# The forget gate's four columns computed with the first query chunk of the third layer

## The chip, the cores and the metric

The kernel runs on one core of one Trainium2 chip. The metric is the device time of one launch in microseconds (us), the median of the runs. Engines are named as the profile names them: PE is TensorE's matmul, PEld its load of the stationary operand, DVE is VectorE, ACT is ScalarE, POOL is GpSimd, SP is SyncE, which here only issues DMAs. ACTq and SPq are the DMA issues of those two queues.

## What is computed

Four transformer layers follow one another on 512 tokens of 1024 features, in float32. The change touches the third, called the even layer. Cut to what matters, its reference is:

```python
hn = rms_norm(h, norm_g)                       # [512, 1024]
proj = hn @ w_in                               # qa ka va qb kb vb, f_logit (4 columns), z
qa, ka = rope(rms_norm(qa)), rope(rms_norm(ka))
oa = diff_attention(qa..., ka..., va, lam)
cum_logf = cumsum(log_sigmoid(f_logit + b_forget), axis=1)
ob = fox_attention(norm(qb), norm(kb), vb, cum_logf)   # scores get cum_logf[q] - cum_logf[k]
h = h + (concat(rms_norm(oa), ob) * silu(z)) @ w_out
```

`f_logit` is four of the 4100 columns of the projection, one for each head of `fox_attention`. Only the second half of the layer's attention uses what is made of it.

## The kernel before

Every product is made of three TensorE passes (`mm3`, L236): both operands are split into a rounded part and a remainder, and high x high, high x low and low x high are summed in PSUM. Weights come in chunks of 256 columns. `weights` (L210) loads a chunk with two DMAs of 512 KB on SP into one of three `raw` buffers, and splits it in four pieces of two feature blocks: ACT makes `wh`, DVE or POOL makes `wl`. There are 8 `wh` and 8 `wl` buffers, so two chunks fit.

`quad` (L269) computes a chunk for all 512 tokens with the tokens stationary: 4 token tiles x 8 feature blocks x 3 passes = 96 matmuls of 256 moving columns into one PSUM buffer `A`. There are two `A` buffers of two banks each, and four single banks: three with the tag `B`, one with the tag `F`. `proj_tok` (L242) runs the token tiles outermost unless `step` is given; with `step=1` the feature blocks are outermost. `head_norm` (L165) copies the sums to SBUF on ACT and normalises each head, `rope` (L185) rotates.

`even` (L1289) opens with constants in `lp`, the layer's pool, whose memory was used before it by the pools of the stage ahead (`xr1`, `plv`). Then `proj_group` (L1095) makes chunk q, chunk k, chunk v and two gate blocks (`gates2`) one after another, each in the next `A` buffer; `forget` (L1115) makes the forget gate; four groups of attention follow, with the next `proj_group` as filler work for PE. The gate blocks are computed features-stationary with 512 moving columns.

`forget` loads its 1024 x 4 weights on ACT's queue, splits them, and runs 8 feature blocks x 3 passes = 24 matmuls with 4 stationary columns and 512 moving ones into bank `F`, which leaves the four heads on four partitions. A chain of ACT and DVE instructions and a scan along the tokens follows, a store of the sums to DRAM for the second half, and four transposes.

The stage ahead is the end of layer two: `w_out` adds its output to the residual in two pairs of token tiles, `feat_pair` (L392) normalises and transposes each pair into `h2h` and `h2l` (the operands of chunk q), and `ple_values` (L1367) computes 2 chunks x 4 token tiles x 6 = 48 matmuls of 512 columns in banks `F` and `B`, copies each result out (`pv`, two buffers, in pool `plv`) and stores it to DRAM (`pw_d`, L1385).

The order of the work on each engine is not written by hand. A scheduler takes the instructions in program order as their priority, and moves one ahead when it is ready earlier; each engine then runs its list in order. A pool whose memory overlaps an earlier pool's waits until the earlier one is released.

Of the kernel before, what the change touches and what calls it, by code (L numbers as in the profile page):

```python
# [9 lines left out]
F32 = mybir.dt.float32  # L10
F32R = mybir.dt.float32r
# [18 lines left out]
class Kern:  # L30
# [38 lines left out]
    def A(self):  # L69
        return self.tl(self.ps, [128, 1024], "A", 2)  # L70
# [91 lines left out]
        self.nc.scalar.activation(out=t, in_=ps, func=AF.Tanh, scale=0.5)  # L162
        self.nc.vector.scalar_tensor_tensor(out=out, in0=t, scalar=1.0, in1=ps, op0=ALU.add, op1=ALU.mult)

    def head_norm(self, ps, H, d):  # L165

        nc = self.nc
        T = ps.shape[1]
        if T == 4:
            x = self.T4([128, T, H * d])  # L170
            nc.scalar.copy(out=x, in_=ps)
            ps = x
        sq = self.T4([128, T, H * d])
        nc.scalar.activation(out=sq, in_=ps, func=AF.Square, scale=d ** -0.5)
        ss = self.sml(T * H)
        nc.vector.tensor_reduce(out=ss.rearrange("p (t h) -> p t h", t=T),
                                in_=sq.rearrange("p t (h d) -> p t h d", d=d), axis=AX.X, op=ALU.add)
        r = self.rstd(ss, T * H)
        xn = ps.rearrange("p t (h d) -> p t h d", d=d)
        nc.vector.tensor_tensor(out=xn, in0=xn,  # L180
                                in1=r.rearrange("p (t h) -> p t h", t=T).unsqueeze(3).to_broadcast([128, T, H, d]),
                                op=ALU.mult)
        return xn
# [678 lines left out]
    def mla_load(self, pool, src):  # L862
        G = self.mla_tiles(pool, 1, 2)
        for x, d in zip((G[0], G[1], f32(G[2])), src):
            self.nc.sync.dma_start(out=x, in_=d)
        return G

    def mla_attn(self, box, att, G, g, g_d, gT):
        st = {}

        def stacks(e):
            q, k, _ = G[g]
            st[e] = [self.qk_any(lambda t: x[:, t, e, :], 6, 96, self.tl(box["mat"], [96, 2, 768], "qk", 4, F32R))
# [5 lines left out]
        def gate(e, pr):  # L879
# [4 lines left out]

        items = self.dense_items(score, lambda e, j: G[g][2][:, j, e].rearrange("p e d -> p (e d)"), gate,
                                 lambda pr: gT[g][:, 256 * pr:256 * pr + 256], att, g == 3)
# [197 lines left out]
        nc.gpsimd.tensor_copy(out=C[:, :, rot:d], in_=g[:, rot:d].unsqueeze(1).to_broadcast([128, 4, d - rot]))  # L1084
        return C, S, rot

    def proj_heads(self, X, W, out, d, tab):

        xn = self.head_norm(self.quad(X, W, 256), 256 // d, d)
        if isinstance(tab, tuple):  # L1090
            self.rope(out, xn, tab[0], tab[1], 0, tab[2])
        else:
            self.gain_heads(out, xn, tab)

    def proj_group(self, X, w, cols, pool, d, tq, tk, z):  # L1095

        H = 256 // d
        q = self.tl(pool, [128, 4, H, d], "q")
        k = self.tl(pool, [128, 4, H, d], "k")
        v = self.tl(pool, [128, 4, 2, 2, 128], "v", 2, F32R)  # L1100
        self.proj_heads(X, self.weights(w[cols[0]]), q, d, tq)
        self.proj_heads(X, self.weights(w[cols[1]]), k, d, tk)
        self.v_split(v, self.quad(X, self.weights(w[cols[2]]), 256).rearrange("p t (h d) -> p t h d", h=2))
        if z is not None:
            self.gates2(X, self.weights(w[cols[3]]), z)
        return q, k, v
# [5 lines left out]
            nc_ = self.nc.vector if b else self.nc.gpsimd  # L1112
            nc_.tensor_tensor(out=z[b], in0=z[b], in1=t, op=ALU.mult)

    def forget(self, X, fp, cq, nc_d):  # L1115
        nc, I = self.nc, self.I
        wf = fp.tile([128, 8, 4], F32, name="wf")
        nc.scalar.dma_start(out=wf, in_=I["w_forget"])
        wfh, wfl = fp.tile([128, 8, 4], F32R, name="wfh"), fp.tile([128, 8, 4], F32R, name="wfl")
        self.split(wf, wfh, wfl)  # L1120
        bf = fp.tile([4, 1], F32, name="bf")
        nc.scalar.dma_start(out=bf, in_=I["b_forget_2"])
        p = self.B()
        for k in range(8):
            self.mm3(p[0:4, :], wfh[:, k, :], wfl[:, k, :], X[0][:, k, :], X[1][:, k, :], k == 0, k == 7)
        f, e, cum = (self.T4([4, 512]) for _ in range(3))
        nc.vector.tensor_scalar(out=f, in0=p[0:4, :], scalar1=bf, scalar2=None, op0=ALU.add)
        nc.scalar.activation(out=e, in_=f, func=AF.Abs)
        nc.scalar.activation(out=e, in_=e, func=AF.Exp, scale=-1.0)
        nc.scalar.activation(out=e, in_=e, func=AF.Ln, bias=1.0)  # L1130
        nc.vector.tensor_scalar(out=f, in0=f, scalar1=0.0, scalar2=None, op0=ALU.min)
        nc.vector.tensor_tensor(out=f, in0=f, in1=e, op=ALU.subtract)
        nc.vector.memset(e, 1.0)
        nc.vector.tensor_tensor_scan(out=cum, data0=e, data1=f, initial=0.0, op0=ALU.mult, op1=ALU.add)
        nc.vector.tensor_scalar(out=f, in0=cum, scalar1=-1.0, scalar2=None, op0=ALU.mult)
        nc.sync.dma_start(out=nc_d, in_=f)
        pc = self.B()
        for t in range(4):
            nc.tensor.transpose(out=pc[:, 4 * t:4 * t + 4], in_=cum[:, 128 * t:128 * t + 128], identity=self.ident[0:4, 0:4])
        nc.vector.tensor_copy(out=cq, in_=pc[:, 0:16])  # L1140
# [148 lines left out]
    def even(self, X, close_x, lp, zt, fold, nc_d):  # L1289
        nc, I = self.nc, self.I  # L1290
        w = I["even_w"]
        gq = self.gain_row(lp, "qn_a_2", "gqa", 0.125)
        gk = self.gain_row(lp, "kn_a_2", "gka")
        te = self.rot_table(lp, 0)
        TQ = self.partial_tables(lp, te, gq, 16, 64)
        TK = self.partial_tables(lp, te, gk, 16, 64)
        gqb = self.gain_row(lp, "qn_b_2", "gqb", float(np.float32(128 ** -0.5)))
        gkb = self.gain_row(lp, "kn_b_2", "gkb")
        li = 0.8 - 0.6 * math.exp(-0.3 * 0)
        sub = self.gain_row(lp, "subln_g_2", "sub", (1.0 - li) * 0.5)  # L1300
        cm = lp.tile([128, 512], F32, name="cmask")
        nc.scalar.dma_start(out=cm, in_=I["causal"])
        cq = lp.tile([128, 16], F32, name="cq")
        nlam = self.lam(lp)
        zg = lambda g: zt[2 * g:2 * g + 2]
        cols = lambda g: [c + g for c in (0, 2, 4, 12)] if g < 2 else [c + g - 2 for c in (6, 8, 10, 14)]
        with self.filler(True):
            G = self.proj_group(X, w, cols(0), lp, 64, TQ, TK, zg(0))
        self.forget(X, lp, cq, nc_d)
        for g in range(4):  # L1310
            if g < 2:
                self.pipeline(self.diff_items(G, lp, cm, nlam, sub, zg(g)))
                fold(*((0, 1) if g == 0 else (2,)))
            else:
                nck = {}

                def bias(h, i, g=g, nck=nck):
                    if h not in nck:
                        nck[h] = self.tl(lp, [128, 512], "nck", 2)
                        hh = 2 * (g - 2) + h  # L1320
                        nc.sync.dma_start(out=nck[h], in_=nc_d[hh:hh + 1, :].to_broadcast([128, 512]))
                    n = 128 * (i + 1)
                    b = self.T4([128, n])
                    c = 4 * i + 2 * (g - 2) + h
                    nc.scalar.activation(out=b, in_=nck[h][:, 0:n], func=AF.Identity, bias=cq[:, c:c + 1])
                    nc.gpsimd.tensor_tensor(out=b[:, n - 128:n], in0=b[:, n - 128:n], in1=cm[:, 384:512], op=ALU.add)
                    return b

                self.pipeline(self.causal_items(G, lp, zg(g), bias, True))
            if g < 3:  # L1330
                with self.filler(True):
                    G = self.proj_group(X, w, cols(g + 1), lp, 64 if g < 1 else 128, TQ if g < 1 else gqb,
                                        TK if g < 1 else gkb, zg(1) if g < 1 else None)
        with self.filler(True):
            for g in (2, 3):
                self.late_gates(X, self.weights(w[12 + g]), zg(g))
        close_x()
# [419 lines left out]
def chunks(w, n=256):  # L1757

    K, N = w.shape
    return np.ascontiguousarray(w.reshape(K // 128, 128, N // n, n).transpose(2, 1, 0, 3))  # L1760


def layout(inp):
    A = np.ascontiguousarray
# [4 lines left out]
    d = {}  # L1769
# [20 lines left out]
    cols = np.concatenate([heads(512, 2, p64), np.arange(640, 768), heads(0, 8, p64), np.arange(768, 3328)])  # L1790
# [2 lines left out]
    d["conv_w"] = A(g["conv_w"][0].reshape(3, 4, 128).transpose(2, 1, 0))  # L1793
    ev = g["w_in_even_2"][0]
    d["even_w"] = chunks(np.concatenate([ev[:, 0:3072], ev[:, 3076:4100]], 1))
    d["w_forget"] = A(ev[:, 3072:3076].reshape(8, 128, 4).transpose(1, 0, 2))
    d["b_forget_2"] = A(g["b_forget_2"].reshape(4, 1))
    d["even_wo"] = chunks(g["w_out_even_2"][0])
    d["odd_w"] = chunks(g["w_in_odd_2"][0])
# [14 lines left out]
    z = np.zeros((128, 128), f)  # L1814
# [28 lines left out]
```

## Time and profile before

| | |
|---|---|
| median of 3 runs | 1543.21 us (1541.46 to 1546.2) |
| the profiled execution | 1542.88 us, span 1541.1 us |
| granted TensorE clock, mean | 0.991 |
| PE / PEld / DVE / ACT / POOL busy | 96% / 89% / 67% / 55% / 36% of the span |
| DMA | 168.20 MB, mean 109 GB/s |

Matmuls are pipelined: the length of one in the profile (0.39 us for 512 columns) is longer than the distance to the next one's start (0.23 us), so what PE can do is read from start to start. Shares of busy time hide short idle stretches; where it matters, starts are read one by one.

### The profile page before, as it was taken

How to read it: one execution, taken by the hardware profiler on the slowest of the kernel's cores; microseconds unless marked ns; L12 is line 12 of the kernel's file. 1: busy time of each engine (PE TensorE's matmuls, PEld its weight loads, DVE VectorE, ACT ScalarE, POOL GpSimd, SP SyncE). 2: the span in 40 equal slices, each digit the busy share in tenths (PEclk: the TensorE clock that was granted, in tenths of full speed). 3: DMA queues.
4: the chain of work that ended last, by engine and by line, in shares of the span. 5: the costliest groups of instructions: out<-in, count | busy, mean ns of one | idle time of the engine just before them, and what ended most of it. 6: DMA issues, size and time to landing. Idle time of an engine off the chain costs nothing.

```text
span 1541.1 us, 28602 instructions
## 1 busy us (share of the span) xinstructions
PE 1483.3 (96%) x10760; PEld 1367.7 (89%) x10760; DVE 1039.1 (67%) x2123; ACT 845.0 (55%) x1759; POOL 551.4 (36%) x650
## 2 busy tenths in 40 slices
PE   5999999989999989999999999999999999999998
PEld 3789888877998989888889989998899989998998
DVE  6777887888886377777755358887644456555544
ACT  6545555689997154465653446566533534454422
POOL 1533534567675024222322244335301244443100
PEclk8999999999999999999999999999999999999999
DMA  8343564121120431222334432112434431222323
GB/s 308 116 131 120 185 207 157 45 104 33 63 70 25 153 119 66 96 97 83 102 129 149 136 114 92 61 56 96 144 103 148 139 105 69 69 71 78 126 90 110
DMA packets 60685, 168.20 MB, mean 109 GB/s; under 512 B 9890, under 2 KB 18530, under 8 KB 60546
## 3 DMA queue, kind: packets, MB, share of 16 engines
q1 hardware_dynamic: 54768, 163.52, 31.1%
q10 hardware_dynamic: 5778, 2.84, 0.7%
q8 instruction: 85, 1.39, 0.4%
q14 instruction: 54, 0.44, 0.1%
HBM read 144.06 MB, written 22.28 MB: 108 GB/s over the span
## 4 chain that ended last, share of the span: by engine, by line
PE 81%; DVE 7%; ACT 4%; DMA 3%; issue 2%; POOL 2%; ACTq 0%; SPq 0%; DVEq 0%; POOLq 0%
PE A L240 17%; PE A L238 17%; PE A L239 16%; PE B L524 3%; PE F L238 3%; PE F L239 3%; PE F L240 3%; PE F L595 2%; PE B L238 2%; PE B L239 2%; PE B L240 2%; DVE wl L232 2%; PE B L996 1%; PE B L388 1%; PE B L1168 1%
## 5 line engine op out<-in xcount | busy, mean ns | idle before, releaser
L229 ACT CAST wh<-raw 128x512 fp32r<-128x512 f32 (+1 forms) x380 | 227.1, 615 | 220.9 <-PE A L240 147.3
L232 DVE TENSOR_TENSOR wl<-raw,wh 128x512 fp32r<-128x512 f32 (+1 forms) x316 | 230.7, 744 | 99.2 <-ACT wh L229 96.6
L481 POOL TENSOR_SCALAR P<-P,s 128x768 f32<-128x768 f32 (+3 forms) x192 | 151.4, 794 | 183.0 <-DVE s L1264 37.5
L144 DVE TENSOR_TENSOR PTl<-B,PTh 128x512 fp32r<-128x512 f32 (+2 forms) x208 | 127.9, 632 | 43.9 <-ACT PTh L143 31.4
L232 POOL TENSOR_TENSOR wl<-raw,wh 128x512 fp32r<-128x512 f32 x64 | 87.3, 1365 | 155.8 <-ACT wh L229 139.2
L138 POOL TENSOR_TENSOR s8f<-s8f,mhalf 128x4 f32<-128x4 f32 (+2 forms) x53 | 61.5, 1161 | 221.0 <-DVE s8f L137 122.2
L143 ACT CAST PTh<-B 128x512 fp32r<-128x512 f32 (+2 forms) x208 | 108.2, 545 | 58.1 <-PE B L524 26.8
L238 PE MATMUL A<-wh,mh 128*128 128x256 f32 x480 | 136.6, 285 | 2.9 <-ACT mh L143 2.9
L239 PE MATMUL A<-wl,mh 128*128 128x256 f32 x480 | 136.0, 284 | 0.0
L240 PE MATMUL A<-wh,g 128*128 128x256 f32 x408 | 115.6, 285 | 1.4 <-DVE g L144 1.4
L238 PE MATMUL A<-wh,h4h 128*128 128x256 f32 x384 | 109.1, 285 | 0.0
L239 PE MATMUL A<-wl,h4h 128*128 128x256 f32 x384 | 108.9, 284 | 0.0
L240 PE MATMUL A<-wh,h4l 128*128 128x256 f32 x384 | 108.8, 285 | 0.0
L240 PE MATMUL A<-wh,h2l 128*128 128x256 f32 x384 | 108.1, 283 | 0.0
L238 PE MATMUL A<-wh,h2h 128*128 128x256 f32 x384 | 108.0, 282 | 0.0
L239 PE MATMUL A<-wl,h2h 128*128 128x256 f32 x384 | 108.0, 282 | 0.0
L238 PEld LDWEIGHTS A<-wh,mh 128*128 128x128 f32 x480 | 92.0, 192 | 4.2 <-ACT mh L143 3.3
L239 PEld LDWEIGHTS A<-wl,mh 128*128 128x128 f32 x480 | 91.9, 192 | 0.1
L524 PE MATMUL B<-ident,P 128*128 128x128 f32 x592 | 86.3, 274 | 4.5 <-DVE PTl L144 2.4
L240 PEld LDWEIGHTS A<-wh,g 128*128 128x128 f32 x408 | 78.0, 192 | 1.8 <-DVE g L144 1.8
L490 ACT ACTIVATE P<-A,s 128x768 f32<-128x768 f32 (+1 forms) x96 | 73.2, 765 | 7.4 <-DVE s L488 4.7
L524 PEld LDWEIGHTS B<-ident,P 128*128 128x128 f32 x592 | 67.5, 141 | 9.1 <-POOL P L481 2.5
(523 smaller groups left out, 4927.3 us busy)
## 6 DMA issues: line engine op xcount, KB each, us to landing
raw<-mod_w SPq DMA_DIRECT2D x32, 512.0 KB
raw<-even_w SPq DMA_DIRECT2D x32, 512.0 KB
raw<-odd_w SPq DMA_DIRECT2D x32, 512.0 KB
raw<-cd_w SPq DMA_DIRECT2D x26, 512.0 KB
mraw<-mod_w SPq DMA_DIRECT2D x16, 512.0 KB
raw<-w_ple_gate SPq DMA_DIRECT2D x16, 512.0 KB
raw<-ab_wg SPq DMA_DIRECT2D x8, 512.0 KB
raw<-ab_wo SPq DMA_DIRECT2D x8, 512.0 KB
```

The source lines that it names most:

```text
L138: self.nc.gpsimd.tensor_tensor(out=ms, in0=ms, in1=self.mhalf[:, 0:n], op=ALU.pow)
L143: self.nc.scalar.copy(out=hi, in_=src)
L144: self.nc.vector.tensor_tensor(out=lo, in0=src, in1=f32(hi), op=ALU.subtract)
L229: nc.scalar.copy(out=hi, in_=r)
L232: eng.tensor_tensor(out=lo, in0=r, in1=f32(hi), op=ALU.subtract)
L238: mm(out=out, lhsT=xh, rhs=wh, start=start, stop=False)
L239: mm(out=out, lhsT=xh, rhs=wl, start=False, stop=False)
L240: mm(out=out, lhsT=xl, rhs=wh, start=False, stop=stop)
L481: self.nc.gpsimd.tensor_scalar(out=P, in0=P, scalar1=s, scalar2=0.0, op0=ALU.mult, op1=ALU.add)
L490: nc.scalar.activation(out=P[:, u, :], in_=S[:, u, :], func=AF.Exp, bias=m[:, u:u + 1], scale=1.0, accum_out=s[:, u:u + 1])
L524: nc.tensor.transpose(out=pt[:, j, u, :], in_=b, identity=self.ident)
L595: nc.tensor.matmul(out=O, lhsT=vst(e, j), rhs=pts[j // 2][w][:, j % 2], start=w + j == 0, stop=w == 1 and j == nk - 1)
```

## The change

The four columns are appended to the first query chunk, which becomes a chunk of 260 columns (`even_w0`). Its loads become three DMAs (3, 3 and 2 feature blocks) and its split eight pieces of one block. The chunk takes both `A` buffers, two token tiles each, with one bank for each token tile, and runs with the feature blocks outermost. DVE copies the last four columns of each token tile into `lt`, a new tile in `lp`; ACT copies the other 256. `forget` then gets its sums by transposing `lt` (tokens x 4) four times into bank `F`. The chain behind is as before. The loading, the split and the 24 matmuls of `forget` are gone.

```diff
-    def head_norm(self, ps, H, d):
+    def head_norm(self, ps, H, d, copy=True):
...
-        if T == 4:
+        if T == 4 and copy:
...
+    def quad_more(self, X, W, more):
+
+        n = W[0][1].shape[2]
+        ps = [self.A().rearrange("p (t n) -> p t n", t=2)[:, :, 0:n] for _ in range(2)]
+        self.proj_tok([p[:, i] for p in ps for i in range(2)], X, W, (0, 128, 256, 384), step=1)
+        x = self.T4([128, 4, 256])
+        for t, p in zip((0, 2), ps):
+            self.nc.vector.tensor_copy(out=more[:, t:t + 2, :], in_=p[:, :, 256:n])
+            self.nc.scalar.copy(out=x[:, t:t + 2, :], in_=p[:, :, 0:256])
+        return x
...
+        if more is None:
+            self.proj_heads(X, self.weights(w[cols[0]]), q, d, tq)
+        else:
+            self.proj_heads(X, self.weights(self.I["even_w0"]), q, d, tq, more)
...
-    def forget(self, X, fp, cq, nc_d):
+    def forget(self, lt, fp, cq, nc_d):
+
         nc, I = self.nc, self.I
-        wf = fp.tile([128, 8, 4], F32, name="wf")
-        nc.scalar.dma_start(out=wf, in_=I["w_forget"])
-        wfh, wfl = fp.tile([128, 8, 4], F32R, name="wfh"), fp.tile([128, 8, 4], F32R, name="wfl")
-        self.split(wf, wfh, wfl)
         bf = fp.tile([4, 1], F32, name="bf")
         nc.scalar.dma_start(out=bf, in_=I["b_forget_2"])
         p = self.B()
-        for k in range(8):
-            self.mm3(p[0:4, :], wfh[:, k, :], wfl[:, k, :], X[0][:, k, :], X[1][:, k, :], k == 0, k == 7)
+        for t in range(4):
+            nc.tensor.transpose(out=p[0:4, 128 * t:128 * t + 128], in_=lt[:, t, :], identity=self.ident)
...
+        lt = lp.tile([128, 4, 4], F32, name="lt")
         with self.filler(True):
-            G = self.proj_group(X, w, cols(0), lp, 64, TQ, TK, zg(0))
-        self.forget(X, lp, cq, nc_d)
+            G = self.proj_group(X, w, cols(0), lp, 64, TQ, TK, zg(0), lt)
+        self.forget(lt, lp, cq, nc_d)
```

## Rows read from the trace of the kernel before

**Rows 1.** Stretches of 20 us: length, busy time (instructions) per engine, granted clock, DMA share, GB/s

```profile
845.00:865.00 20.00, 20.00 (x152) 19.09 (x151) 10.22 (x22) 9.33 (x21) 2.40 (x3) 1.00 0.36 119
...
905.00:925.00 20.00, 20.00 (x156) 17.71 (x155) 9.10 (x14) 9.61 (x14) 3.87 (x3) 1.00 0.31 104
```

**Rows 2.** Timeline of PE, forget's matmuls and their neighbours: start, length, instruction

```profile
897.10 0.39 PE L238 MATMUL F<-h2h,wfh 128*4 128x512 f32 x1
...
899.18 0.40 PE L238 MATMUL F<-h2h,wfh 128*4 128x512 f32 x1
899.69 0.50 PE L238 MATMUL A<-h2h,wh 128*128 128x512 f32 x1
...
908.63 0.28 PE L238 MATMUL A<-wh,h2h 128*128 128x256 f32 x1
```

**Rows 3.** The chain that ended last, before the second gate block: start, length, what

```profile
893.25 2.91 POOL s16f L138
...
896.18 2.31 DVE t4f L180
898.50 1.14 DVE v L144
```

**Rows 4.** The same chain, ahead of the first instruction on the layer's pool

```profile
875.24 0.97 ACT pv L1384 x2
...
876.59 4.89 DMA pw_d<-pv
...
881.58 0.36 ACTq L129
```

**Rows 5.** Waits of the SP queue, 860 to 905: who for whom, total, times, longest

```profile
SPq L1073 <- DMA pw_d<-pv: 4.5, 1, 4.5
```

**Rows 6.** Timelines of PE: twelve 288-column passes in a row; nine transposes

```profile
48.26 0.29 PE L240 MATMUL A<-wh,hTl 128*128 128x288 f32 x1
...
49.73 0.29 PE L239 MATMUL A<-wl,hTh 128*128 128x288 f32 x1
...
855.03 1.14 PE L388 MATMUL B<-ident,t4f 128*128 128x128 f32 x9
```

**Rows 7.** Stretches, only instructions on tile h2h (columns as in Rows 1, no POOL)

```profile
845.60:863.30 17.70, 11.71 (x65) 9.75 (x65) 5.24 (x12) 4.17 (x10) 1.00 0.33 105
863.30:875.00 11.70, 6.13 (x34) 5.37 (x35) 0.00 (x0) 0.00 (x0) 1.00 0.40 140
```

**Rows 8.** Timeline of PE around the matmuls of ple_values (tile p2h or p2l)

```profile
863.13 0.39 PE L240 MATMUL B<-whf,p2l 128*128 128x512 f32 x1
863.35 0.28 PE L240 MATMUL A<-wh,h2l 128*128 128x256 f32 x1
...
866.06 0.28 PE L239 MATMUL A<-wl,h2h 128*128 128x256 f32 x1
866.18 0.40 PE L238 MATMUL F<-whf,p2h 128*128 128x512 f32 x1
...
873.95 0.28 PE L239 MATMUL A<-wl,h2h 128*128 128x256 f32 x1
```

**Rows 9.** Timelines of SP and ACT, stores of ple_values and a copy waiting for one

```profile
862.78 3.04 SPq L1385 DMA_DIRECT2D pw_d<-pv  x3
...
864.89 0.59 ACT L1384 COPY pv<-B 128x512 f32<-128x512 f32 x1 [0.60 <-DMA pw_d<-pv]
872.75 1.01 ACT L171 COPY t4f<-A 128x1024 f32<-128x1024 f32 x1
```

**Rows 10.** The odd layer at the same place: PE timeline, and stretches as in Rows 1

```profile
1253.32 0.73 PE L238 MATMUL A<-h4h,wh 128*128 128x512 f32 x1 [3.09 <-DVE v L144]
...
1253.00:1254.00 1.00, 0.68 (x2) 0.59 (x3) 1.00 (x4) 0.00 (x0) 0.00 (x0) 0.71 0.65 238
1254.00:1255.00 1.00, 1.00 (x4) 0.82 (x3) 0.86 (x2) 0.00 (x0) 0.00 (x0) 0.50 0.25 102
...
1256.00:1257.00 1.00, 1.00 (x4) 0.82 (x3) 0.00 (x0) 0.41 (x1) 0.52 (x1) 0.58 0.00 0
```

More of the change, by code (lines that the diff above doesn't have):

```diff
@@ L1085, in partial_tables, with proj_heads @@
         return C, S, rot
-    def proj_heads(self, X, W, out, d, tab):
-        xn = self.head_norm(self.quad(X, W, 256), 256 // d, d)
+    def proj_heads(self, X, W, out, d, tab, more=None):
+        if more is None:
+            xn = self.head_norm(self.quad(X, W, 256), 256 // d, d)
+        else:
+            xn = self.head_norm(self.quad_more(X, W, more), 256 // d, d, False)
         if isinstance(tab, tuple):
@@ L1093, in proj_heads, with proj_group @@
             self.gain_heads(out, xn, tab)
-    def proj_group(self, X, w, cols, pool, d, tq, tk, z):
+    def quad_more(self, X, W, more):
[7 more added lines that the diff above has]
+        return x
+    def proj_group(self, X, w, cols, pool, d, tq, tk, z, more=None):
         H = 256 // d
@@ L1100, in proj_group @@
         v = self.tl(pool, [128, 4, 2, 2, 128], "v", 2, F32R)
-        self.proj_heads(X, self.weights(w[cols[0]]), q, d, tq)
+        if more is None:
+            self.proj_heads(X, self.weights(w[cols[0]]), q, d, tq)
+        else:
+            self.proj_heads(X, self.weights(self.I["even_w0"]), q, d, tq, more)
         self.proj_heads(X, self.weights(w[cols[1]]), k, d, tk)
@@ L1795, in layout @@
     d["even_w"] = chunks(np.concatenate([ev[:, 0:3072], ev[:, 3076:4100]], 1))
-    d["w_forget"] = A(ev[:, 3072:3076].reshape(8, 128, 4).transpose(1, 0, 2))
+    d["even_w0"] = chunks(np.concatenate([ev[:, 0:256], ev[:, 3072:3076]], 1), 260)[0]
     d["b_forget_2"] = A(g["b_forget_2"].reshape(4, 1))
```

## The prediction

> **What bounds the kernel now.** PE does, and nearly everywhere; so an edit is worth what it takes from PE's own list, unless it makes PE wait. I read the views in this order. First the stretches of 20 us around the change: the columns PE of 845 to 925 read 20.00 of 20 at a granted clock of 1.00, while ACT and DVE are about half busy [rows 1]. Then PE's starts one by one, since busy shares hide short waits: forget's first ten matmuls start at 897.10 to 899.18, that is 2.08 us for nine steps, 0.231 us each; then PE waits from about 899.41 to 899.69, 0.28 us, and the second gate block runs; the other fourteen matmuls end where the next group begins at 908.63 [rows 2]. Third the chain of waits, which is PE except in one place: ahead of 899.69 stand the power of chunk k's norm on POOL, k's scaling on DVE and, behind these in DVE's order, the evacuation of chunk v, whose buffer the second gate block needs [rows 3]. So forget's first ten matmuls are not pure cost: they fill a wait. Last I asked what the same chain waited for before that, because the change adds a tile to the layer's pool: the last two results of ple_values are copied at 875.24, their stores leave, the last takes 4.89 us, and only then does ACT's queue issue the layer's first load, at 881.58 [rows 4]. SP's first load into the layer's pool waited for the same stores, 4.5 us [rows 5]. Two queues and two tiles, one event: the layer's pool opens as a whole when the last store has landed, some 881.5.
>
> **What the change does, part by part.**
>
> Removed: 24 matmuls x 0.231 = 5.55 us of PE [rows 2]. Removed with them: a load and a split of 32 columns, on ACT and DVE, which have idle time there [rows 1]; I take nothing for these.
>
> Added to the chunk: four columns on 96 passes. A pass of 288 columns takes (49.73 - 48.26) / 11 = 0.134 us [rows 6], one of 256 takes (866.06 - 863.35) / 23 = 0.118 us [rows 8]. The difference, over 32 columns, is 0.0005 us a column; 4 x 96 of them are 0.19 us.
>
> Added to forget: four transposes with 4 stationary columns. The nearest row has 128: nine in 1.14 us [rows 6], so four cost 0.51 us at most. Nothing excludes zero; I take 0.51. They stand on PE's list, with nothing to hide them. The chain behind them has until the second half of the layer. Bank F comes free earlier, so the first attention work may start earlier; PE's stretch after the change is full already [rows 1], so I give that nothing.
>
> Loads and split: three loads instead of two on SP, eight casts instead of four on ACT, eight subtractions on DVE and POOL. All this is ahead of the chunk, in the stretch where ACT is busy 9.33 of 20 [rows 1]. But eight pieces fill all eight weight buffers, where half of them held chunk k before. So k's pieces can be split only as q's blocks are finished for all four token tiles. Covered by the hold below; without that cover k's first piece would still be ready while PE finishes q.
>
> The hold, which decides. The chunk takes both A buffers. A buffer is free again when ACT has copied 256 columns of each token tile and DVE has copied the four into `lt`. ACT's copy can go at once. DVE's copy cannot: `lt` lies in the layer's pool, which is closed until the last store of ple_values has landed. Before, nothing that PE waited for was written to that pool so early. Now both accumulators stay taken; chunk k, chunk v and the gate blocks all need one, and forget itself needs `lt`. PE is left with chunk q and ple_values.
>
> When does PE run out? Before, until 873.95, where the last matmul of ple_values has been issued [rows 8], PE ran chunk q, part of chunk k and all of ple_values. Tile h2h is in two of three passes of a chunk: 65 + 34 rows x 1.5 = 148 passes by 875 [rows 7], 139 by 873.95 at 0.118 each, 43 more than chunk q's 96. Without these 43 PE is through at 873.95 - 43 x 0.118 + 0.19 = 869.1.
>
> When does k start? The last matmul of ple_values can end at 869.1 at the earliest. Two gaps that k's passes filled may push it out: 2.83 us between its two chunks, while the second chunk's weights are split (863.35 to 866.18), and part of the 7.8 us that the second chunk took, 24 x 0.231 = 5.55 being its own work [rows 8]. So 869.1 to some 872.8; I take 870.5, as chunk q's last tiles fill half of the first gap. From there to the store: 0.97 for two copies and 0.38 to issue is the least, 2.64 (873.95 to 876.59) the most [rows 4, 8]; I take 2.0. The store: 4.89 [rows 4], or 2.11 where a copy waited for an earlier one (862.78 to 864.89) [rows 9]; I take 2.9, nearer to the lower, since the loads of weights are held up too. Then two copies of eight values a partition on DVE; the row of 1024 values is 1.14 [rows 3], nothing is the other end, and I take 0.4 for both with the hand-over. k starts at 872.8 to 881, most likely at 875.8, and PE is idle for 3.7 to 12 us, most likely 6.7.
>
> The clock. In the odd layer PE stood idle for 3.09 us and then ran at half clock (1.2 of 2.4 GHz): the granted shares 0.71, 0.50, 0.50 and 0.58 of four slices of 1 us lose 1.7 us [rows 10]. I add 1.7 once.
>
> What is late next: behind k the order is unchanged, but the wait before the second gate block is gone. k's norm is done before v's passes end, so DVE is free for v's evacuation; that gains the 0.28 us.
>
> Sum: -5.55 - 0.28 + 0.19 + 0.51 + 1.7 + 6.7 = +3.3 us, with ends of +0.3 and +8.6. On the profiled execution, 1542.88 (span 1541.1 and 1.8 around it), this gives 1546.2; the median lies 0.3 above that execution, so 1546.5, with 1543.5 to 1551.8 as this case's own range.
>
> The Trainium skill, page "Perfetto Trace Analysis", section "Optimizing Tensor Performance", says under Matmuls that independent groups of matmuls should rotate through different PSUM banks, so that the evacuation of one overlaps the next. It speaks against giving both buffers to one chunk. The trace of before agrees: chunk q was copied out at 872.75 for 1.01 us while chunk k's passes went on in the other buffer [rows 8, 9]. By that rule alone k would wait for one exposed copy of 512 columns, 0.59 us [rows 9], and the third rival below would lose 0.6 of its gain; the hold above is another thing, as it waits for memory and not for a copy.
>
> **The rivals.**
>
> The pool opens no earlier than before. If ple_values keeps its pace, because its order on each engine, its two result buffers and the loads ahead of its last store stay as they are, k starts at 881.5 + 0.4 and PE is idle for 12.8 us: +9.4, 1552.6. For it: the store's 4.89 us is a DMA's, not PE's. Against: PE reaches ple_values' second chunk earlier once k's passes are out of its way. It decides from the point where k starts later than 877.2: there the loss passes 0.3%.
>
> `lt` is not held, and the wait at the second gate block takes the place of the ten matmuls that filled it, as in the odd layer, which has no forget gate and stands idle just there [rows 10]. Then only fourteen of the matmuls are gained: -14 x 0.231 + 0.19 + 0.51 + 1.7 = -0.8, 1542.4. For it: rows 3 and 10. Against: rows 4 and 5.
>
> `lt` is not held, and v is evacuated in time: the whole PE saving, -5.55 - 0.28 + 0.19 + 0.51 = -5.1, 1538.1. It needs both the pool open and another order on DVE.
>
> **How the numbers follow.** About 0.3% (4.6 us: below 1538.6 or above 1547.8) is what a measurement of this kernel can tell from no change. The forecast's case has 0.68, the late pool 0.12, the wait at the gate block 0.10, the whole saving 0.06; 0.04 is left for a different order elsewhere. In the forecast's case about a third lies above 1547.8. That gives slower 0.12 + 0.22 = 0.34, faster 0.06, same 0.60. The range takes in the forecast's own range, the wait at the gate block below and the late pool above, and leaves out the whole saving: 1541.5 to 1553.
>
> **What would show it.** In the profile after: DVE's copy into `lt` waits, and starts right behind the landing of the last store of ple_values; PE idle for 4 to 12 us just before chunk k, with that copy named as releaser; half clock for some 3 us behind it; chunk q's passes at about 0.12 us; no wait at the second gate block; next group's first chunk at about 912. The prediction is wrong if `lt` is written while ple_values still runs, or if PE has other work to fill the hold.

## The result, and the profile after

The changed kernel takes 1552.54 us (median of 7 runs, 1549.51 to 1557.03), the kernel before 1544.50 us in the same comparison (7 runs, 1541.17 to 1546.62): a ratio of 1.0053, with an interval of 1.0041 to 1.0066. That is 8.0 us slower where +3.3 us was forecast; the median lies 0.5 us inside the upper end of the range. The execution with a profile took 1550.11 us, span 1548.3 us, mean granted clock 0.985 (before 0.991).

Two lengths carry the comparison, because single executions of one and the same list of work differ by some us long before the change (chunk q starts at 845.67 before and at 842.59 after). The first group is read on PE's timeline from the first pass on `h2h` to the first pass of the next group's first chunk: 62.96 us before (845.67 to 908.63, [rows 2]), 74.13 after. The even layer is read from the first pass on `h2h` to the first on `h4h`: 351.8 before, 362.2 after.

What PE waited for in the even layer, first in the kernel after, then in the kernel before (engine, tile written, line <- engine, tile and line that released it: total us, times, longest):

```profile
PE F L1140 <- DVE lt L1106: 7.2, 1, 7.2
PE A L238 <- ACT t4f L1107: 3.7, 1, 3.7
...
PE A L238 <- DVE v L144: 0.3, 1, 0.3
```

```profile
PE B L238 <- DVE PTl L144: 0.6, 1, 0.6
PE B L1168 <- ACT g L1281: 0.4, 1, 0.4
```

Two new waits, 10.9 us, both ahead of chunk k. The first is the forecast hold. The chain that ended last, as the kernel after has it between the last results of ple_values and the layer's first loads (start, length, what):

```profile
865.40 5.03 DMA pw_d<-pv
...
870.53 0.59 ACT pv L1400
...
871.13 0.60 ACT pv L1400
...
871.74 2.08 DMA pw_d<-pv
...
874.00 0.35 ACTq L129
...
876.32 1.51 ACTq L1317
```

The store of 865.40 takes 5.03 us and holds one of the two `pv` buffers; the last two results can be copied only then (870.53, 871.13), and the last store (2.08 us) lands at 873.82. At 874.0 the pool is open. The second wait is seen on the timeline of the kernel after (start, length, engine, line, instruction, [idle before <- releaser]):

```profile
874.05 0.24 DVE L1106 COPY lt<-A 128x8 f32<-128x8 f32 x2 [10.80 <-DMA pw_d<-pv]
874.27 1.01 PE L1140 MATMUL F<-ident,lt 128*4 128x128 f32 x4 [7.18 <-DVE lt L1106]
...
878.36 0.59 ACT L1107 COPY t4f<-A 128x512 f32<-128x512 f32 x1 [6.64 <-DMA gqb<-qn_b]
...
878.84 0.59 ACT L1107 COPY t4f<-A 128x512 f32<-128x512 f32 x1
879.00 0.58 PE L238 MATMUL A<-wh,h2h 128*128 128x256 f32 x1 [3.71 <-ACT t4f L1107]
```

`lt` is written 0.05 us after the pool opens. The other reader of the same accumulator, ACT's copy of the 256 columns, comes 4.3 us later: on ACT it stands behind seven issues of the layer's constants (874.00 to 878.32), which wait for the same pool. Only at 879.00 does chunk k have an accumulator.

The clock, in stretches of 2 us of the kernel after (columns as in [rows 1]; granted clock third from the end):

```profile
866.00:868.00 2.00, 1.08 (x5) 0.56 (x3) 0.00 (x0) 0.00 (x0) 0.00 (x0) 1.00 0.84 251
...
872.00:874.00 2.00, 0.00 (x0) 0.00 (x0) 0.00 (x0) 0.00 (x0) 0.00 (x0) 0.50 0.68 255
...
878.00:880.00 2.00, 1.00 (x4) 1.01 (x5) 0.29 (x1) 1.61 (x3) 1.17 (x5) 0.50 0.15 39
...
884.00:886.00 2.00, 2.00 (x16) 2.00 (x15) 1.44 (x5) 1.97 (x4) 0.00 (x0) 0.81 0.00 0
886.00:888.00 2.00, 2.00 (x19) 2.00 (x18) 0.09 (x1) 1.97 (x3) 1.94 (x1) 1.00 0.00 0
```

PE has been idle since 867.09; the granted clock is at half (1.2 of 2.4 GHz) when k starts and comes back between 884 and 886.

An account of the even layer can be made from these views, and was made for every kernel below: idle is the sum of the idle times that PE's timeline shows; clock is the sum, over stretches of 1 us, of PE's busy time x (1 - granted clock); work is what is left. Before: 351.8 = 1.0 idle + 0.0 clock + 350.8 work. After: 362.2 = 12.9 + 3.4 + 345.8. So PE's own work did fall by 5.0 us, and 11.9 us of idle time and 3.4 us of half clock came in.

### The profile page after: what moved, and what is told of

It reads as the page before. It is cut to its first block, busy times and chain, and to the rows that moved or that the text cites. A ratio compares the mean times of both kernels' runs of the same rounds, so it can differ in the third digit from the quotient of the medians.

```text
span 1548.3 us, 28579 instructions
## 1 busy us (share of the span) xinstructions
PE 1483.0 (96%) x10740; PEld 1370.6 (89%) x10740; DVE 1043.1 (67%) x2126; ACT 846.3 (55%) x1763; POOL 551.0 (36%) x652
## 4 chain that ended last, share of the span: by engine, by line
PE 78%; DVE 8%; DMA 5%; ACT 4%; issue 3%; POOL 2%; ACTq 0%; SPq 0%; DVEq 0%; POOLq 0%
PE A L240 16%; PE A L238 16%; PE A L239 16%; PE B L524 3%; PE F L238 3%; PE F L239 3%; PE F L240 3%; PE F L595 2%; DVE wl L232 2%; PE B L238 2%; PE B L239 2%; PE B L240 2%; DMA raw<-mod_w 1%; PE B L996 1%; PE B L388 1%
## 5 line engine op out<-in xcount | busy, mean ns | idle before, releaser
L229 ACT CAST wh<-raw 128x512 fp32r<-128x512 f32 (+2 forms) x384 | 227.7, 611 | 213.1 <-PE A L240 141.5
L232 DVE TENSOR_TENSOR wl<-raw,wh 128x512 fp32r<-128x512 f32 (+2 forms) x318 | 232.4, 746 | 83.9 <-ACT wh L229 81.4
L138 POOL TENSOR_TENSOR s8f<-s8f,mhalf 128x4 f32<-128x4 f32 (+2 forms) x53 | 62.2, 1174 | 225.4 <-DVE s8f L137 201.9
L232 POOL TENSOR_TENSOR wl<-raw,wh 128x512 fp32r<-128x512 f32 (+1 forms) x66 | 86.6, 1314 | 137.1 <-ACT wh L229 124.0
L238 PE MATMUL A<-wh,h2h 128*128 128x256 f32 (+1 forms) x384 | 109.9, 286 | 3.7 <-ACT t4f L1107 3.7
L240 PE MATMUL A<-wh,h2l 128*128 128x256 f32 (+1 forms) x384 | 109.3, 285 | 0.0
L239 PE MATMUL A<-wl,h2h 128*128 128x256 f32 (+1 forms) x384 | 109.3, 285 | 0.0
L238 PEld LDWEIGHTS A<-wh,h2h 128*128 128x128 f32 x384 | 73.4, 191 | 4.7 <-ACT t4f L1107 4.2
```

What stands on the lines that cost most here:

```text
L138: self.nc.gpsimd.tensor_tensor(out=ms, in0=ms, in1=self.mhalf[:, 0:n], op=ALU.pow)
L229: nc.scalar.copy(out=hi, in_=r)
L232: eng.tensor_tensor(out=lo, in0=r, in1=f32(hi), op=ALU.subtract)
L238: mm(out=out, lhsT=xh, rhs=wh, start=start, stop=False)
L239: mm(out=out, lhsT=xh, rhs=wl, start=False, stop=False)
L240: mm(out=out, lhsT=xl, rhs=wh, start=False, stop=stop)
```

## The experiments

The theory after the result: chunk k waits because `lt` lies in a pool that is closed, and longer than that because ACT's copies of chunk q stand behind VectorE's copies and behind the constants' issues. Rival 1: the layout (one chunk in both accumulators) does it, wherever `lt` lies. Rival 2: the loss comes from another order of the work further down.

All results in one table; the parts of each are below. Ratio: to the kernel before, run beside it. First group, even layer, idle, clock and work are us, from the profiled execution, read as above.

| kernel | ratio (95% interval) | first group | even layer | idle | clock | work |
|---|---|---|---|---|---|---|
| before | 1 | 63.0 | 351.8 | 1.0 | 0.0 | 350.8 |
| after | 1.0053 (1.0041 to 1.0066) | 74.1 | 362.2 | 12.9 | 3.4 | 345.8 |
| e1 `lt` in an open pool | 0.9993 (0.9978 to 1.0008) | 63.4 | 357.7 | 8.5 | 3.1 | 346.2 |
| e2 ACT's copies first | 1.0056 (1.0042 to 1.0071) | 67.8 | 361.9 | 12.7 | 1.8 | 347.4 |
| e3 layout alone | 0.9996 (0.9987 to 1.0006) | 63.4 | 352.3 | 1.2 | 0.0 | 351.1 |
| e4 one forget matmul | 1.0031 (1.0020 to 1.0042) | 59.5 | 354.8 | 8.5 | 0.0 | 346.4 |
| e5 = e4 + order | 1.0029 (1.0018 to 1.0039) | 59.4 | 354.4 | 7.3 | 1.6 | 345.5 |
| e6 = e2 + order | 1.0050 (1.0034 to 1.0065) | 68.1 | 360.8 | 12.1 | 1.5 | 347.3 |
| e7 = e1 + order | 0.9993 (0.9977 to 1.0008) | 63.3 | 356.2 | 7.2 | 3.4 | 345.6 |
| e8 = e1 + v first | 0.9973 (0.9961 to 0.9986) | 64.6 | 354.5 | 6.2 | 3.2 | 345.1 |
| e9 = before + v first | 1.0022 (1.0007 to 1.0036) | 65.5 | 355.6 | 3.7 | 1.7 | 350.1 |
| e10 = after + v first | 1.0064 (1.0041 to 1.0087) | 74.8 | 364.6 | 14.8 | 3.4 | 346.4 |
| e11 = e4 + v first | 1.0062 (1.0044 to 1.0080) | 65.7 | 359.6 | 10.0 | 3.0 | 346.6 |
| e12 = e8 + late transposes | 0.9986 (0.9969 to 1.0002) | 64.4 | 353.8 | 7.3 | 1.6 | 344.9 |

### e1: `lt` in a pool that is open

```diff
-        lt = lp.tile([128, 4, 4], F32, name="lt")
+        lt = self.const.tile([128, 4, 4], F32, name="lt")
```

> The changed kernel with one line different: `lt` lies in the pool of constants, which is open from the start, instead of the layer's pool. Theory (the hold): k waits only because `lt` cannot be written before the last store of ple_values has landed, and what needs the two accumulators stands behind that. Then the copies into `lt` run at some 862, as soon as chunk q is through, PE has no idle stretch before chunk k, no half clock there, and the time falls 9 to 13 us below the changed kernel's 1552.5: between -0.8 us (the wait at the second gate block takes the place of the ten matmuls) and -5.1 us against the kernel before, a ratio of 0.9967 to 0.9995. Rival 1 (the layout: a chunk that takes both accumulators leaves the next without one, wherever `lt` lies): the wait ahead of k stays, ratio about 1.005. Rival 2 (what is lost is lost further down, by another order in the layer): ratio about 1.005, without an idle stretch ahead of k.

Ratio 0.9993: 9.3 us below the changed kernel (0.0060 of 1543). `lt` is written while ple_values still runs; timeline of VectorE:

```profile
847.92 0.17 DVE L1106 COPY lt<-A 128x8 f32<-128x8 f32 x1 [2.77 <-PE A L240]
860.34 0.15 DVE L1106 COPY lt<-A 128x8 f32<-128x8 f32 x1
```

and PE has no wait ahead of chunk k: one line takes both waits of the changed kernel away, so the pool of `lt` is their cause. What e1 does not do is gain the 5 us of work that PE has less. In its place PE waits for the evacuation of chunk v, twice:

```profile
PE A L238 <- DVE v L144: 5.4, 2, 2.8
```

The first of the two (2.62 us) stands ahead of the second gate block, as the second rival of the prediction had it; the other (2.79 us) stands at the same place in the second group, where nothing was foreseen. Rival 2 is half right: the waits of the changed kernel are not further down, but without them the even layer is still 5.9 us longer than before, by what is lost there.

So of the 9.3 us only 4.5 lie in the even layer (362.2 to 357.7). The rest is a second effect of the same line, which has nothing to do with the hold: passes of 256 columns start closer together elsewhere in the kernel. In the odd layer, which none of the edits touches, 138 passes on `h4h` and `h4l` run in a row without a wait. The first and the last of them on PE's timeline, in the kernel before and in e1:

```profile
1227.60 0.27 PE L238 MATMUL A<-wh,h4h 128*128 128x256 f32 x1
...
1244.03 0.28 PE L240 MATMUL A<-wh,h4l 128*128 128x256 f32 x1
```

```profile
1227.29 0.28 PE L238 MATMUL A<-wh,h4h 128*128 128x256 f32 x1
...
1243.43 0.28 PE L240 MATMUL A<-wh,h4l 128*128 128x256 f32 x1
```

That is 16.43 us against 16.14 for 137 steps, 0.1199 us each against 0.1178. The changed kernel has 0.1199, and so have all kernels here but those with `lt` in the constants' pool (e1, e7, e8, e12), which all have 0.1178. By the same account as above, PE's work outside the even layer is 1112.9 to 1116.5 us in these four and 1119.2 to 1123.9 in the other ten, some 7 us less. For e1, 5.9 us more in the even layer and some 7 less outside it make some -1 us against the kernel before; -1.1 was measured. A total of one of the four therefore can't be set against another kernel's total to price the hold; the even layer can.

### e2: ACT's copies written down first

```diff
         for t, p in zip((0, 2), ps):
-            self.nc.vector.tensor_copy(out=more[:, t:t + 2, :], in_=p[:, :, 256:n])
             self.nc.scalar.copy(out=x[:, t:t + 2, :], in_=p[:, :, 0:256])
+            self.nc.vector.tensor_copy(out=more[:, t:t + 2, :], in_=p[:, :, 256:n])
```

> The changed kernel with two lines exchanged: for each token pair ScalarE's copy of the 256 columns is written down ahead of VectorE's copy of the four; `lt` stays in the layer's pool. Theory (the hold has two parts, and the second is that ScalarE's copies wait for VectorE's of the same accumulator and so stand behind seven DMA issues of the layer's constants): ScalarE's copies move ahead of these issues, to some 862, the wait for `lt` to about 874 stays, and k starts some 0.5 us after it instead of 4.9: about 4.4 us less than the changed kernel, +3 to +4 us against the kernel before (ratio 1.002 to 1.0026). If the order of the two copies does not matter (ScalarE's copies are late for a reason of their own), k still starts at about 879 and the ratio stays 1.005.

The mechanism came as expected, the time did not. ACT's copies run early and PE waits for `lt` alone (timelines of ACT, VectorE and PE):

```profile
857.20 0.59 ACT L1106 COPY t4f<-A 128x512 f32<-128x512 f32 x1 [4.18 <-PE A L240]
868.88 0.59 ACT L1106 COPY t4f<-A 128x512 f32<-128x512 f32 x1
...
880.66 0.24 DVE L1107 COPY lt<-A 128x8 f32<-128x8 f32 x2 [4.00 <-DMA pw_d<-pv]
880.88 0.58 PE L238 MATMUL A<-wh,h2h 128*128 128x256 f32 x1 [7.18 <-DVE lt L1107]
...
964.79 0.50 PE L238 MATMUL A<-h2h,wh 128*128 128x512 f32 x1 [2.77 <-DVE v L144]
```

So it is the order in which the two readers of one accumulator are written down that put ACT's copy behind VectorE's, and with it behind the seven issues: 3.71 us of wait, and 6.3 us of the first group (74.1 to 67.8). But the ratio is 1.0056: the rest of the layer, 362.2 - 74.1 = 288.1 us in the changed kernel, is 294.1 here, with a wait of 2.77 us for chunk v in the second group that the changed kernel does not have.

### e3: the layout alone

The first query chunk of the kernel before takes both accumulators, feature blocks outermost, with 256 columns and no copy into `lt`; the forget gate is untouched.

> The kernel before with the layout of the change alone: the first query chunk takes both accumulators, feature blocks outermost, with its 256 columns and without the four; the forget gate's matmuls stay where they were and nothing of the chunk is written to the layer's pool early. Theory (the hold is `lt`'s): no wait ahead of k, within 1.5 us of the kernel before (ratio 0.999 to 1.001). Rival 1 (the layout itself makes k late): +5 to +13 us, ratio 1.003 to 1.008.

Ratio 0.9996, idle 1.2 us: rival 1 falls. The Trainium skill, "Perfetto Trace Analysis", section "Optimizing Tensor Performance", has independent groups of matmuls rotate through PSUM banks; giving one chunk both accumulators goes against that, and by that rule alone, the prediction says, chunk k would wait 0.6 us. The trace of e3 does not show even that: while ACT copies the second accumulator, PE goes on with matmuls of ple_values in bank `F`, and then with chunk k (timelines of ACT and PE).

```profile
867.42 0.59 ACT L1106 COPY t4f<-A 128x512 f32<-128x512 f32 x1 [1.88 <-PE A L240]
867.58 0.40 PE L238 MATMUL F<-whf,p2h 128*128 128x512 f32 x1
...
868.97 0.28 PE L240 MATMUL A<-wh,h2l 128*128 128x256 f32 x1
```

The passes of this chunk also price the four columns at an equal layout: between neighbouring starts 0.118 us with 256 columns (e3) and 0.120 us with 260 (after), both as medians, since a few steps of 0.2 to 0.3 us next to the transposes of the second token pair pull the averages up. That is 0.2 us for 96 passes.

### e4: one forget matmul instead of 24

```diff
-        for k in range(8):
-            self.mm3(p[0:4, :], wfh[:, k, :], wfl[:, k, :], X[0][:, k, :], X[1][:, k, :], k == 0, k == 7)
+        nc.tensor.matmul(out=p[0:4, :], lhsT=wfh[:, 0, :], rhs=X[0][:, 0, :], start=True, stop=True)
```

> The kernel before with one of the forget gate's 24 matmuls kept and 23 left out (its decay values are then not the reference's); all else stays. It measures what those matmuls are worth on PE's list. If they are pure cost: -23 x 0.231 = -5.3 us, ratio 0.9966. If the wait for the evacuation of chunk v takes the place of the ten ahead of the second gate block: the other fourteen alone, -3.2 us, ratio 0.9979, with a wait of about 2 us there and perhaps half clock behind it, which would leave -1.5 us, ratio 0.999.

Neither: taking 23 matmuls out of the kernel before makes it 0.31% slower. In the first group it does what the second expectation says (59.5 us, 3.4 less), and PE's work in the layer falls by 4.4 us; then PE waits 7.5 us more than before, which is more than the work that went:

```profile
PE A L238 <- DVE v L144: 4.8, 2, 2.8
PE F L1138 <- DVE t L1133: 1.1, 1, 1.1
PE B L469 <- ACT qk L451: 1.1, 1, 1.1
```

How little room there is behind the first group, the kernel before shows in stretches that the prediction did not read (columns as in [rows 1]):

```profile
910.00:930.00 20.00, 20.00 (x172) 19.85 (x171) 9.70 (x15) 9.51 (x15) 5.48 (x3) 1.00 0.25 85
930.00:950.00 20.00, 20.00 (x156) 19.32 (x156) 18.72 (x47) 15.19 (x31) 10.44 (x8) 1.00 0.15 53
```

From 930 to 950 VectorE is busy for 18.72 of 20 us and ACT for 15.19. The stretches of [rows 1] end at 925, and in the last of them VectorE has half its time left.

### e5, e6, e7: another place for chunk v's evacuation in the second group

The scheduler lays the lists out anew whenever an instruction changes. In e4 VectorE's half of chunk v's evacuation in the second group starts 6.8 us after ACT's half (945.44 to 952.21), in the kernel before 2.9 us (948.42 to 951.27); e1 and e2 are like e4. These three kernels add one edit, which queues the gate chunk's split behind it (the order of the list alone, no wait is added). The code is cut: it stands under a condition that holds in the second group alone.

```diff
-            self.gates2(X, self.weights(w[cols[3]]), z)
+            with self.tc.issue_after(ev.ins):
+                W = self.weights(w[cols[3]])
+            self.gates2(X, W, z)
```

> The kernel of e4 (one forget matmul instead of 24) with one more edit: in the second group, the split of the gate chunk's weights on VectorE is queued behind the evacuation of chunk v. In e4 the first group became 3.4 us shorter and the rest of the even layer 6.5 us longer, with a new wait of 2.79 us for that evacuation. Theory (order): the loss in the rest is the place of the evacuation in VectorE's list, which the scheduler chose anew when the first group's times moved. Then the wait in the second group goes, the rest of the layer is back near 289 us (295.3 in e4, 288.8 in the kernel before), and the time is 2.5 to 3.5 us below the kernel before, ratio 0.9977 to 0.9984. Rival (no slack): VectorE is so full in the second group that PE waits for it whatever the order; the ratio stays at 1.002 to 1.004.

> The kernel of e2 (ScalarE's copies of chunk q written down first, `lt` still in the layer's pool) with the same queueing in the second group as e5. Theory: in e2 the earlier copies did take 6.3 us from the first group (67.8 us against 74.1 in the changed kernel), and another order in the second group lost them again (294.1 us for the rest of the layer against 288.1). With the order put right the rest is near 289 and what remains is the wait for `lt` alone: +3.5 to +5 us against the kernel before, ratio 1.0023 to 1.0033. Rival (the place of ScalarE's copies is worth nothing): ratio 1.005 or more.

> The kernel of e1 (`lt` in a pool that is open) with the same queueing in the second group as e5. Theory: the wait of 2.79 us in the second group and the half clock behind it go, the rest of the even layer falls from 294.3 to about 289 us, and the first group stays as in e1 with the wait of 2.6 us ahead of the second gate block: -4 to -6 us against e1, ratio 0.995 to 0.998 against the kernel before. Rival (no slack on VectorE): as e1, ratio 0.999.

All three ratios stay where they were: 1.0029, 1.0050, 0.9993. The wait for v in the second group went (the 1.9 us that are left in e5 are the first group's), and one for ACT's operands of the attention came, in e5:

```profile
PE B L469 <- ACT qk L451: 2.9, 1, 2.9
PE A L238 <- DVE v L144: 1.9, 1, 1.9
```

and in e6, on PE's timeline:

```profile
955.11 0.50 PE L469 MATMUL B<-qk,qk 128*128 128x256 f32 x2 [2.69 <-ACT qk L451]
```

So the place of this one evacuation was not the cause of the loss; what came is what the rival "no slack" foresaw, for this order. That VectorE and ACT together are too full there for any order is argued from the stretch from 930 to 950, and not shown.

### e8, e9, e10, e11: chunk v first, in four kernels

Chunk v's evacuation goes ahead of chunk k's rotation and of the gate chunk's split, in both groups with 64-wide heads (code cut).

```diff
-        self.proj_heads(X, self.weights(w[cols[1]]), k, d, tk)
-        self.v_split(...)
+        xn = self.head_norm(self.quad(X, self.weights(w[cols[1]]), 256), H, d)
+        ev = self.v_split(...)
+        with self.tc.issue_after(ev.ins):
+            self.rope(k, xn, tk[0], tk[1], 0, tk[2])
+            W = self.weights(w[cols[3]])
```

> The kernel of e1 with VectorE's evacuation of chunk v queued ahead of chunk k's rotation and ahead of the split of the gate chunk's weights, in both groups with 64-wide heads. Theory: now neither the hold nor a wait for v takes the place of the 24 matmuls, in the first group or in the second; the whole saving stays: -5.5 for the matmuls, +1.2 for the wider passes as the changed kernel's trace has them (0.130 against 0.118 us each) and +0.5 to +1.0 for the four transposes make -3.3 to -3.8 us against the kernel before, ratio 0.9975 to 0.998, and lower by what the earlier part of e1 gained. Rival (the next engine is late at once): a wait of the same size elsewhere in the layer, ratio 0.999 to 1.0.

> The kernel before, with e8's order on VectorE (chunk v is evacuated ahead of chunk k's rotation and of the gate chunk's split in the two groups with 64-wide heads) and without the change. It splits e8's gain. If e8's gain is the matmuls' and the order only keeps it: within 1.5 us of the kernel before (ratio 0.999 to 1.001), since that kernel has 0.3 us of waits in these two groups. If the order alone is the gain: ratio 0.997.

> The changed kernel, `lt` in the layer's pool as the change has it, with e8's order on VectorE. It prices the hold at one and the same order, against e8. Theory: the hold is 11 us of idle PE and 3 us of half clock, of which the matmuls give back 3.5: +8 to +11 us over e8, ratio 1.003 to 1.0045 against the kernel before. Rival (the hold is made up for later, because the engines behind PE catch up in it): within 4 us of e8, ratio below 1.0005.

> The kernel of e4 (one forget matmul instead of 24) with e8's order on VectorE. Theory (order): the waits of 2.0 us in the first group and 2.8 in the second go, and the 5.3 us of matmuls come out as a gain: ratio 0.9965 to 0.998. Rival (no slack: what follows the forget gate waits for ScalarE and VectorE in any order, as e5 showed when the wait went from v's evacuation to ScalarE's operands for attention): ratio 1.001 to 1.003.

e8, with `lt` in the open pool, is the one kernel that is faster than both: 0.9973, about what was expected of it, but by luck, since the reason given for it is only half there. The waits for v are gone, but PE now waits for the forget gate's scan:

```profile
PE F L1163 <- DVE t L1158: 3.2, 1, 3.2
PE A L240 <- DVE wl L232: 1.2, 1, 1.2
```

and its profiled execution has the even layer at 354.5 us, 2.7 more than before, and what follows it, up to the last matmul, at 334.6 against 339.5. That part, which the change does not touch, is shorter by a wait that is 1.1 us shorter, by a half clock that is absent in this execution (1.7 us), and by 2.2 us of faster passes. The gain of 4.2 us is the faster passes of all kernels with `lt` in the constants' pool (some 7 us, see e1) less the 2.7 us of the even layer; it is not a gain of the even layer.

e9 shows that the same order does harm to the kernel before (1.0022, with a new wait of 2.1 us for the scan). e10 prices the hold at e8's order: 10.1 us by the even layer (364.6 against 354.5). The totals, 1.0064 against 0.9973, say 14 us, but here too some 7 of them are the faster passes. Its two waits are those of the changed kernel:

```profile
PE F L1149 <- DVE lt L1106: 7.0, 1, 7.0
PE A L238 <- ACT t4f L1107: 3.5, 1, 3.5
```

e11 repeats e4 at this order and again is slower, by 0.40% against e9 (1.0062 against 1.0022). Again PE's work falls (3.5 us) and its waits grow (6.3 us):

```profile
PE A L238 <- DVE v L144: 4.6, 1, 4.6
PE A L238 <- DVE g L163: 3.4, 2, 2.1
```

The wait for v in the first group, which this order was to remove, has grown from 2.01 us (e4) to 4.59. VectorE is not full there. Its half of v's evacuation now stands ahead of k's rotation, but still behind the scaling of k's norm (L180), and this waits for a power that GpSimd computes in 2.92 us (timelines of ACT, VectorE and PE):

```profile
888.74 1.01 ACT L143 CAST v<-A 128x1024 fp32r<-128x1024 f32 x1
...
891.19 2.28 DVE L180 TENSOR_TENSOR t4f<-t4f,s16f 128x1024 f32<-128x1024 f32 x1 [2.93 <-POOL s16f L138]
893.39 1.21 DVE L144 TENSOR_TENSOR v<-A,v 128x1024 fp32r<-128x1024 f32 x1
...
894.66 0.80 PE L238 MATMUL A<-h2h,wh 128*128 128x512 f32 x1 [4.59 <-DVE v L144]
```

ACT's half is done at 889.75. VectorE's starts at 893.39, behind the scaling, before which VectorE does nothing for 2.93 us. The kernel before has the same chain [rows 3]. An order with v's evacuation ahead of the scaling was not tried; so e11 does not decide between order and want of room in the first group.

### e12: the last transposes of the forget gate later

e8, with the four transposes of the summed decays and the copy behind them written down behind the first attention group; the sums lie in a buffer of the tag `nck` until then.

> The kernel of e8, with the last four transposes of the forget gate (and the copy behind them) written down behind the first attention group instead of ahead of it; the sums that they turn lie in a buffer of the second half's until then. In e8 PE stands idle for 3.16 us ahead of these transposes, at 911.62, since the scan on VectorE is not through. Theory: this wait goes, -3 to -4.5 us against e8, ratio 0.9945 to 0.9955 against the kernel before. Rival (the wait moves to the next operand of the second group): as e8, ratio 0.997.

The rival: the wait for the scan goes, and one for the evacuation of a gate block, at the start of the second group, takes its place.

```profile
PE A L238 <- DVE g L163: 3.8, 2, 3.2
```

Ratio 0.9986 with an interval that reaches over 1; no gain over e8 is shown.

## Why the prediction was right or wrong, step by step

**The hold.** Right, and shown: `lt` waits for the pool, and moving `lt` alone takes the 10.9 us of waits ahead of chunk k away (e1). PE was put at its end at 870.5, or 24.8 us after chunk q's first pass, and is at its end at 867.09 after a start at 842.59, 24.5 us. The pool was put at some 4.9 us behind that and opens 6.9 us behind (867.09 to 874.0), since a result had to wait for a `pv` buffer held by a store of 5.03 us; the first wait is 7.18 us where 6.7 was taken for the whole hold.

**The hand-over: the step that failed.** "ACT's copy can go at once", and 0.4 us for both copies and the hand-over. From `lt`'s copies (874.05) to chunk k (879.00) it is 4.95 us. The prediction looked at what each copy needs and not at what stands ahead of it on its engine: ACT's copies were ordered behind VectorE's of the same accumulator (e2: with the lines exchanged the later of them runs at 868.88, 11.8 us before `lt` is written), and so fell behind the constants' issues, which the same pool held up. The rows were there: ACT's issues begin at 881.58 in the kernel before [rows 4].

**The clock.** 1.7 us was taken from a wait of 3.09 us [rows 10]; after 10.9 us in two waits, with four transposes in between, the even layer loses 3.4 us.

**PE's own work.** -5.55 + 0.19 + 0.51 = -4.85 was forecast, and the account gives -5.0. The four columns cost 0.2 us (e3 against after), as forecast; the expectation of e8, which takes 1.2 us for them, read the average steps of 0.130 us and not the undisturbed ones. The four transposes stand between the two waits, where they cost nothing (PE is idle for 3.71 us behind them).

**The wait at the second gate block.** Said to be gone, a gain of 0.28; 0.3 us of it is there.

**The sum.** -5.0 + 11.9 + 3.4 = +10.3 us in the even layer of the profiled executions, against +3.3. The medians of the runs differ by 8.0. Of the difference to the forecast, 4.5 us are the hand-over and 1.7 the clock. With these two as forecast the loss would have stayed within 0.3%; it is 0.53%, an outcome that was given 0.34.

**What bounds the kernel.** "PE, and nearly everywhere; so an edit is worth what it takes from PE's own list, unless it makes PE wait": the condition is what matters. In no kernel here did the 3.5 to 5.9 us that PE has less to do come out as an even layer shorter than that of the kernel before: e4 gives back 7.5 us as waits, e1 7.5 and 3.1 us of half clock. Against e9, which has the same order and all 24 matmuls, e8's even layer is 1.1 us shorter for 5.0 us less work. The stretches that the prediction read end at 925 [rows 1]; from 930 to 950 VectorE has 1.3 us of 20 left. Its "20.00 of 20" for PE is also not quite so: the stretch from 885 to 905, with the short wait before the second gate block, reads 19.89.

**The rivals.** "The pool opens no earlier than before" gave 1552.6, and 1552.54 was measured, but by another mechanism, so the agreement is luck, and with it that the median still lies in the range, whose upper end was set by this rival: the pool opens 31.4 us after chunk q's first pass (842.59 to 874.0), 35.9 before (845.67 to 881.58), so it did open 4.5 us earlier. The second rival (`lt` not held, a wait takes the place of the ten matmuls) is e1: its wait of 2.62 us and its half clock are there. That its -0.8 us stands beside a measured -1.1 is luck again: the even layer of e1 is 5.9 us longer, and some 7 us of faster passes elsewhere make up for it. The third (the whole saving) came in no kernel's even layer.

**What stays open.** Why the passes of 256 columns are faster with `lt` in the constants' pool (0.1178 us against 0.1199, e1). That one line does it is shown, as e1 and the changed kernel differ in nothing else; whether it is the place of the other tiles in SBUF, which a tile more in that pool can move, was not tried. The price of the hold, by the even layer alone, is 4.5 us (after against e1) to 10.1 us (e10 against e8). That the engines behind PE make up for a part of the hold, more in one order than in the other, is a reading of these two numbers and no more. And it is open whether another order, v's evacuation ahead of the scaling of k's norm, would keep what PE saves.

## What to carry to other kernels

A small result that is written to a tile of a pool not yet open holds the accumulator, and with it every reader of this accumulator that is ordered behind; put such a tile where memory is open, and ask of each reader what stands ahead of it on its engine's list, DMA issues included. Before work is taken from a full engine, read the busy times of the other engines in the stretches behind the change, not only around it: in this layer, where one of them is nearly as full and chains through other engines end late, the work that went came back as waits. An account of idle, clock and work tells this from one profile, where the total only says that nothing was gained. And before a total is explained, compare the pace of passes that the edit does not touch: here a tile of 64 bytes a partition in another pool changed it by nearly 2%, which gave one kernel a gain and hid a longer even layer in three.

## What was not expected of the hardware

VectorE's instructions can grow while GpSimd works. In e1, timeline of VectorE and GpSimd:

```profile
883.12 0.28 DVE L197 TENSOR_TENSOR q<-q,t2f 128x128 f32<-128x128 f32 x1
...
891.01 3.01 POOL L232 TENSOR_TENSOR wl<-raw,wh 128x512 fp32r<-128x512 f32 x2
891.52 1.37 DVE L196 TENSOR_TENSOR k<-k,t2f 128x128 f32<-128x128 f32 x1
892.82 1.35 DVE L197 TENSOR_TENSOR k<-k,t2f 128x128 f32<-128x128 f32 x1
```

The same 128 x 128 addition takes 0.28 us alone and 1.35 us beside a split on GpSimd. Not every instruction of GpSimd does this: beside the power of a norm (L138) the addition keeps 0.29 and 0.28 us (kernel before, 939.46 and 939.67).

The clock does not fall after every wait of 2 to 3 us: e4 has waits of 2.01 and 2.79 us and loses nothing, e1 has waits of 2.62 and 2.79 us and loses 3.1 us. And single executions differ early: even among the ten kernels with the slower passes, whose work up to there is nearly the same, chunk q's first pass stands between 841.96 (e3) and 849.04 (e2), so that a total of one execution says little about 5 us.
